# Out-projection of a hybrid attention layer by seven block products instead of eight

## The chip, the cores and the metric

The kernel runs on one core of a Trainium2 chip. The metric is the time of one execution on the device in microseconds (us); lower is better. The core has five engines that work side by side, each through its own instructions in order: PE (TensorE, matmuls), DVE (VectorE), ACT (ScalarE), POOL (GpSimd) and SP (SyncE), which here issues every DMA. An instruction waits on semaphores of other engines, and what stands behind it on its engine waits with it.

## The reference, cut to what matters

One layer: a normalised input of 2048 tokens x 1024 goes through one projection, whose columns feed an attention with 8 heads and a gated recurrence with 4 heads. Their gated outputs, 512 columns each, are joined to `y` (2048 x 1024). Then:

```
y = jnp.concatenate([y_mla, y_hg], axis=-1) @ w_out[l]
x = x + y.astype(x.dtype)
...
return rms_norm(x, final_norm_g)
```

All data are float32. Of the layer only this last product, 2048 x 1024 by 1024 x 1024, is computed in another way by the change.

## The kernel before

A matmul here takes operands of 32 bits at reduced precision (`fp32r`). To keep float32 accuracy every operand is cut in a high part (a cast, on ACT) and a low part (value minus high part, on DVE or POOL), and a product is three matmuls, high x high, high x low, low x high: the helper `mm3`, lines L68 to L70. A matmul has 128 x 128 stationary weights and up to 512 columns, so "128x512" is the largest.

The work stands in three phases. Up to some 705 us come the in-projections (weights `wr` loaded in 256 KB pieces, L196, cast and cut at L202 and L203 into `w`) with the recurrence between them. Up to 1268 us comes the attention: for each head and each 256 queries, scores (L854 to L856), softmax (L859 to L870), transposes of the probabilities (L902), their cast and cut (L905, L906), applies to the values (L920, L921), then the head's output `oa` (copied L931, L932, gated L933) stored to DRAM (`y_d`, L935). The recurrence's half of `y` had been stored to the same `y_d` earlier. Last comes the out-projection (L1010 to L1055): 16 blocks of 128 tokens, and for each a load of `yl` from `y_d` (L1020, 512 KB), cast and cut (L1021, L1022), a load of the residual `x` (L1024), two halves of 512 output columns with 8 x 3 matmuls each, an add of the residual from PSUM (L1035), the sum of squares (L1036), the product with the norm's weight (L1040) or a scaling with it (L1047), a scaling (L1046) and a store (L1052). `w_out` is loaded and cut in the last head (`load_wout`, L947 to L960, at step WOUT of that head).

The program's order on each engine is not that of the code: a scheduler simulates the program and writes instructions of every engine in the order in which they could start there. So the first blocks of the out-projection are mixed into the last steps of the attention. DMAs carry one of eight rotating semaphores (`DMAHW0` to `DMAHW7` in rows of the order); each waits for the one eight places before it.

## Time and profile before

| | |
|---|---|
| time, median of 3 runs | 1424.99 us (1424.39 to 1425.21) |
| span of the profiled execution | 1424.0 us |
| PE busy | 1395.9 us, 98% |
| DVE, ACT, POOL busy | 67%, 62%, 33% |
| first out-projection matmul, last apply of the attention, last matmul (start) | 1231.1, 1267.14, 1417.58 us |

The profiled execution is one of its own; its own time is its span, from the first to the last instruction. A share of busy time is an average over all phases. PE's listed durations overlap, since matmuls are pipelined: the time that one counts is read from the distance of starts.

### The profile page before, as it was taken

The numbers are of one execution on the slowest core, as the hardware profiler recorded it, in microseconds if no ns is written. First come the engines' busy times: TensorE is split into PE (matmuls) and PEld (weight loads), VectorE is DVE, ScalarE is ACT, GpSimd is POOL, SyncE is SP. The second block draws the span as 40 slices with busy tenths as digits, with TensorE's granted clock in tenths as the row PEclk, the third lists the DMA queues.
The fourth block names the chain that finished last, engine by engine and source line by source line (L and its number), as shares of the span: only waits on it lengthen the run. The fifth ranks groups of instructions, "written<-read, shape, count | busy, mean of one in ns | idle before, by whom it ended". The sixth has DMA issues, their size and how long they took to land.

```text
span 1424.0 us, 25891 instructions
## 1 busy us (share of the span) xinstructions
PE 1395.9 (98%) x9314; PEld 1271.8 (89%) x9314; DVE 954.6 (67%) x2433; ACT 878.6 (62%) x1796; POOL 464.3 (33%) x635
## 2 busy tenths in 40 slices
PE   8999999999999999999989999999999999999998
PEld 7899879989889988999879999999999998888887
DVE  6547855595645746658389889897889888744333
ACT  6565575456672647345387788778877888732232
POOL 3123613083121522227262425233433425411010
PEclk9999999999999999999989999999999999999999
DMA  6211211214221112111640110000010103244342
GB/s 185 75 48 46 75 52 31 70 38 157 64 60 35 45 60 74 45 42 36 165 106 9 28 23 13 22 15 20 15 27 9 25 24 100 79 137 148 133 148 104
DMA packets 96351, 92.10 MB, mean 65 GB/s; under 512 B 31072, under 2 KB 84576, under 8 KB 96096
## 3 DMA queue, kind: packets, MB, share of 16 engines
q1 hardware_dynamic: 96224, 90.46, 21.7%
q8 instruction: 73, 1.20, 0.4%
q14 instruction: 54, 0.44, 0.1%
HBM read 64.22 MB, written 25.17 MB: 63 GB/s over the span
## 4 chain that ended last, share of the span: by engine, by line
PE 86%; DVE 5%; ACT 3%; POOL 2%; DMA 2%; issue 2%; SPq 0%; POOLq 0%; DVEq 0%; ACTq 0%
PE ps_mm L68 14%; PE ps_mm L69 14%; PE ps_mm L70 14%; PE ps_tp L902 8%; PE ps_a L921 5%; PE ps_a L920 4%; PE ps_mm L854 4%; PE ps_mm L855 4%; PE ps_mm L856 4%; PE ps_b L68 2%; PE ps_b L70 2%; PE ps_b L69 2%; PE ps_b L459 1%; PE ps_a L459 1%; POOL dd L441 1%
## 5 line engine op out<-in xcount | busy, mean ns | idle before, releaser
L68 PE MATMUL ps_mm<-w,hh 128*128 128x256 f32 (+3 forms) x896 | 270.2, 302 | 0.0
L69 PE MATMUL ps_mm<-w,hh 128*128 128x256 f32 (+3 forms) x896 | 265.3, 296 | 0.0
L70 PE MATMUL ps_mm<-w,hl 128*128 128x256 f32 (+3 forms) x896 | 264.2, 295 | 0.0
L906 DVE TENSOR_TENSOR pl<-ps_tp,ph 128x512 fp32r<-128x512 f32 (+1 forms) x288 | 184.4, 655 | 32.9 <-ACT ph L905 32.3
L905 ACT CAST ph<-ps_tp 128x512 fp32r<-128x512 f32 (+1 forms) x288 | 154.1, 565 | 61.5 <-PE ps_tp L902 47.3
L68 PEld LDWEIGHTS ps_mm<-w,hh 128*128 128x128 f32 x896 | 171.4, 191 | 1.0 <-ACT kr L234 0.3
L69 PEld LDWEIGHTS ps_mm<-w,hh 128*128 128x128 f32 x896 | 171.2, 191 | 0.4
L70 PEld LDWEIGHTS ps_mm<-w,hl 128*128 128x128 f32 x896 | 170.6, 190 | 0.1
L902 PE MATMUL ps_tp<-ident,sn 128*128 128x128 f32 x1088 | 168.1, 274 | 0.6 <-ACT sn L868 0.5
L868 ACT ACTIVATE sn<-sn,mx 128x128 f32<-128x128 f32 (+15 forms) x128 | 154.6, 1208 | 21.5 <-DVE mx L863 21.0
L920 PE MATMUL ps_a<-ph,vp 128*128 128x256 f32 x576 | 155.5, 290 | 0.0
L921 PE MATMUL ps_a<-pl,vp 128*128 128x256 f32 x576 | 147.3, 289 | 0.3 <-DVE pl L906 0.2
L441 POOL TENSOR_TENSOR dd<-G 128x512 f32<-128x512 f32 x80 | 92.9, 1166 | 144.0 <-DVE qd L454 109.3
L902 PEld LDWEIGHTS ps_tp<-ident,sn 128*128 128x128 f32 x1088 | 126.9, 140 | 8.5 <-ACT sn L868 1.1
L854 PE MATMUL ps_mm<-k_hi,qh 128*128 128x512 f32 (+3 forms) x320 | 131.1, 410 | 0.3 <-DVE sn L859 0.2
L859 DVE TENSOR_SCALAR_CACHE_REDUCE sn<-ps_mm,mx 128x512 f32<-128x512 f32 (+3 forms) x192 | 111.5, 581 | 10.0 <-PE ps_mm L856 8.3
L856 PE MATMUL ps_mm<-k_hi,ql 128*128 128x512 f32 (+3 forms) x320 | 116.7, 365 | 1.2 <-DVE ql L815 1.2
L855 PE MATMUL ps_mm<-k_lo,qh 128*128 128x512 f32 (+3 forms) x320 | 116.4, 364 | 0.0
L203 DVE SCALAR_TENSOR_TENSOR w<-wr,lng,w 128x256 fp32r<-128x256 f32 (+3 forms) x168 | 88.4, 568 | 39.3 <-ACT w L202 39.3
L921 PEld LDWEIGHTS ps_a<-pl,vp 128*128 128x128 f32 x576 | 109.1, 189 | 6.1 <-DVE pl L906 1.4
L920 PEld LDWEIGHTS ps_a<-ph,vp 128*128 128x128 f32 x576 | 109.0, 189 | 5.8 <-ACT ph L905 0.4
L887 POOL TENSOR_SCALAR gp<-gate,ri 128x64 f32<-128x64 f32 x128 | 56.3, 443 | 174.1 <-DVE ri L870 158.4
(275 smaller groups left out, 3355.3 us busy)
## 6 DMA issues: line engine op xcount, KB each, us to landing
wr<-in_w_in SPq DMA_DIRECT2D x68, 256.0 KB
yl<-y_d SPq DMA_DIRECT2D x16, 512.0 KB
vp<-in_x SPq DMA_DIRECT2D x16, 512.0 KB
out<-sn SPq DMA_DIRECT2D x15, 512.0 KB
xt<-in_x SPq DMA_DIRECT2D x8, 512.0 KB
y_d<-yt SPq DMA_DIRECT2D x16, 256.0 KB
gate<-gate_d SPq DMA_DIRECT2D x8, 512.0 KB
y_d<-oa SPq DMA_DIRECT2D x64, 64.0 KB
```

The costliest lines, as they stand in the source:

```text
L68: PE.matmul(ps, l_hi, r_hi, start=start, stop=False)
L69: PE.matmul(ps, l_hi, r_lo, start=False, stop=False)
L70: PE.matmul(ps, l_lo, r_hi, start=False, stop=stop)
L854: PE.matmul(p[:, :w], qh[:, qs], kh[:, ks], start=True, stop=False)
L855: PE.matmul(p[:, :w], qh[:, qs], kl[:, ks], start=False, stop=False)
L856: PE.matmul(p[:, :w], ql[:, qs], kh[:, ks], start=False, stop=True)
L868: A.activation(sn[:, :nk], sn[:, :nk], AF.Exp, bias=mx[:, kc:kc + 1], scale=-1.0, accum_out=rs)
L902: PE.transpose(tp[:, o:o + 128], prow[i][:, (kb + u) * 128:(kb + u + 1) * 128], ident)
L905: A.copy(ph[:, :w], tp[:, :w])
L906: V.tensor_tensor(pl[:, :w], tp[:, :w], f32(ph[:, :w]), ALU.subtract)
L920: PE.matmul(dst, vv, ph[:, rng], start=st_, stop=False)
L921: PE.matmul(dst, vv, pl[:, rng], start=False, stop=en)
```

## The change

Strassen's scheme in Winograd's form: two blocks of 128 tokens are a pair (8 pairs), `y` of a pair is cut in four quadrants a11, a12, a21, a22 (128 tokens x 512), `w_out` in b11 to b22 (512 x 512). Seven products of sums of quadrants replace eight. The sums of weights are t1 to t4, those of `y` are s1 to s4. Sums of products are not added up by an engine: products accumulate on in PSUM. A first product in bank a is copied by ACT to bank b, the third product is added there, and that is copied on to bank c; a, b, c and e then take further products and DVE adds the banks to the residual. Two matmuls at the start only initialise banks b and c.

`wout_sums` makes the weight sums, in 8 calls for 128 rows x 256 columns of each quadrant: 2 loads of `w_out`, 4 subtracts on POOL, 3 casts on ACT, 3 subtracts on DVE, 7 stores to `w_d` in DRAM. The code hangs the calls on the in-projections. In the last head `load_wout` loads b11, t1, t2, b21, t3, already cut (10 loads of 1 MB); `load_late` loads pair 0's `y` (as `vp`) and b22 and t4 uncut. After the attention pair 0's `y` is loaded a second time (`yr`) into a new pool `op`, for the operands a12, s3, s4 and a22. Tiles of the attention (`ks`, `vs`, `qf`, `qh`, `ql`) move to the pool `big`, which closes at `load_late`. The core of the diff:

```
-WOUT = 4
+WOUT = 3
...
+    def wout_sums(kk, ch):
...
+        ns = slice(ch * 256, ch * 256 + 256)
+        wr = st.tile([128, 2, 2, 256], F32, tag="ws", bufs=1, name="ws")
+        for g in range(2):
+            r0 = g * 512 + kk * 128
+            DMA.dma_start(wr[:, g], w_out[r0:r0 + 128, :].rearrange("p (c n) -> p c n", c=2)[:, :, ns])
+        t = st.tile([128, 2, 256], F32, tag="wt", bufs=1, name="wt")
+        G.tensor_tensor(t[:, 0], wr[:, 0, 1], wr[:, 0, 0], ALU.subtract)
+        G.tensor_tensor(wr[:, 0, 1], wr[:, 1, 1], wr[:, 0, 1], ALU.subtract)
+        DMA.dma_start(w_d["b22"][:, kk, ns], wr[:, 1, 1])
+        G.tensor_tensor(wr[:, 1, 1], wr[:, 1, 1], t[:, 0], ALU.subtract)
+        G.tensor_tensor(t[:, 1], wr[:, 1, 0], wr[:, 1, 1], ALU.subtract)
+        DMA.dma_start(w_d["t4"][:, kk, ns], t[:, 1])
+        for src, names in ((wr[:, :, 0], ("b11", "b21")), (wr[:, :, 1], ("t3", "t2")), (t[:, 0:1], ("t1",))):
+            hl = st.tile([128, 2, 2, 256], F32R, tag="whl", bufs=2, name="whl")
+            n = len(names)
+            A.copy(hl[:, 0, :n], src)
+            V.tensor_tensor(hl[:, 1, :n], src, f32(hl[:, 0, :n]), ALU.subtract)
+            for i, name in enumerate(names):
+                DMA.dma_start(f32(w_d[name][:, :, kk, ns]), f32(hl[:, :, i]))
...
-    merge(U[7:], lat_q(0, hA))
+    merge(U[7:], lat_q(0, hA), sums[0:2])
...
+        return [ops[0], lambda: late("b22", w_d["b22"]),
+                lambda: late("t4", w_d["t4"])] + ops[1:4]
...
+    def late_split(name, kk):
+        hi, lo = wset[name]
+        A.copy(hi[:, kk], f32(lo[:, kk]))
+        G.tensor_tensor(lo[:, kk], f32(lo[:, kk]), f32(hi[:, kk]), ALU.subtract)
...
+    order = (("a11", "b11", "a"), ("s1", "t1", "e"), ("s2", "t2", "b"), ("a12", "b21", "a"),
+             ("s3", "t3", "b"), ("s4", "b22", "c"), ("a22", "t4", "b"))
...
+        def product(i, ns=slice(0, 512)):
+            a, w, bk = order[i]
+            (ah, al), (wh, wl), p = o[a], wset[w], acc[bk][:, ns]
+            for k in range(4):
+                first = i < 2 and k == 0
+                PE.matmul(p, ah[:, k], wh[:, k, ns], start=first, stop=False, skip_group_check=True)
+                PE.matmul(p, ah[:, k], wl[:, k, ns], start=False, stop=False, skip_group_check=True)
+                PE.matmul(p, al[:, k], wh[:, k, ns], start=False, stop=k == 3, skip_group_check=True)
...
+            if i == 0:
+                A.copy(acc["b"], acc["a"])
+            elif i == 1:
+                add(0, H1, acc["e"])
+                add(1, H1, acc["e"])
+            elif i == 2:
+                A.copy(acc["c"], acc["b"])
+            elif i == 3:
+                add(0, H0, acc["a"])
+                done(0, H0, True)
...
+    ys = [{} for _ in range(NBLK // 2)]
+    ys[0] = outs["y0"]
+    rest = operands(0, ys[0])
+    run(rest[:2])
+    rest = rest[5:]
+    run(rest[:1])
+    for name in ("b22", "t4"):
+        for kk in range(4):
+            late_split(name, kk)
+    run(rest[1:])
+    for b in range(NBLK // 2):
+        more = operands(b + 1, ys[b + 1]) if b + 1 < NBLK // 2 else []
+        merge(pair_products(b, ys[b]), more)
```

How the order on the engines moves, first SP early, right after the loads of the rotary tables' inputs (`pi`, `iv`). Names as above; in brackets the semaphores waited for. Before:

```order
L544 DMA pi<-in_positions 128x16x1 [waits DMAHW6_49]
L548 DMA iv<-in_c_inv 128x16 [waits DMAHW7_49]
L196 DMA wr<-in_w_in 128x2x256 [waits DMAHW2_49,DMAHW0_49,DVE_49]
L159 DMA xt<-in_x 128x1024 [waits DMAHW1_49,PE_49]
L159 DMA xt<-in_x 128x1024 [waits DVE_49,PE_49]
```

After (`ws`, `wt`, `whl` are the tiles of `wout_sums`, `wd_...` their places in DRAM):

```order
L551 DMA iv<-in_c_inv 128x16 [waits DMAHW7_49]
L596 DMA ws<-in_w_out 128x2x256 [waits DMAHW0_49]
L596 DMA ws<-in_w_out 128x2x256 [waits DMAHW1_49]
L199 DMA wr<-in_w_in 128x2x256 [waits DMAHW2_49,DVE_49]
L600 DMA wd_b_102<-ws 128x256 [waits DMAHW3_49,DMAHW1_49]
L610 DMA wd_b_96<-whl 256x1x256 [waits DMAHW4_49,DVE_49]
L610 DMA wd_b_99<-whl 256x1x256 [waits DMAHW5_49]
L603 DMA wd_t_101<-wt 128x256 [waits DMAHW6_49,Pool_49]
L610 DMA wd_t_100<-whl 256x1x256 [waits DMAHW7_49,DVE_49]
```

The 72 DMAs of the eight calls fill SP from here up to the stores of the rotary tables (`cs_d`), with the loads `wr` and `xt` between them.

Second, PE at the last applies of the attention. Before:

```order
L68 MATMUL ps_mm<-wo_hi_15277,yh 128x512
L921 MATMUL ps_a<-pl,vp 128x256 [waits DVE_49]
L920 MATMUL ps_a<-ph,vp 128x256
L921 MATMUL ps_a<-pl,vp 128x256
L920 MATMUL ps_a<-ph,vp 128x256 [waits Activation_49]
L921 MATMUL ps_a<-pl,vp 128x256 [waits DVE_49]
L920 MATMUL ps_a<-ph,vp 128x128
L921 MATMUL ps_a<-pl,vp 128x128
L69 MATMUL ps_mm<-wo_lo_15278,yh 128x512
```

After (L949 and L950 are the applies, L1153 to L1155 the three matmuls of a product):

```order
L949 MATMUL ps_a<-ph,vp 128x256 [waits Activation_49]
L950 MATMUL ps_a<-pl,vp 128x256 [waits DVE_49]
L949 MATMUL ps_a<-ph,vp 128x128
L950 MATMUL ps_a<-pl,vp 128x128
L1153 MATMUL ps_mm<-b21s,ah 128x512 [waits DMAHW2_49,Activation_49]
L1154 MATMUL ps_mm<-b21s,ah 128x512
L1153 MATMUL ps_mm<-t3s,ah 128x512 [waits DMAHW4_49,Activation_49]
L1154 MATMUL ps_mm<-t3s,ah 128x512
L1155 MATMUL ps_mm<-b21s,al 128x512 [waits DVE_49]
```

Before, matmuls of the out-projection stand among the applies and right behind them. After, the last eight groups of transposes and applies have none between them, and the next is the fourth product, whose `ah` comes from `yr`.

Third, SP at the same place. Before:

```order
L1024 DMA vp<-in_x 128x1024 [waits DMAHW6_49]
L935 DMA y_d_72<-oa 64x256 [waits DMAHW3_49,Pool_49]
L1020 DMA yl<-y_d_69 128x8x128 [waits PE_49]
L1024 DMA vp<-in_x 128x1024 [waits DMAHW5_49,PE_49]
L1052 DMA out<-sn 128x1024 [waits DVE_49,Activation_49]
L935 DMA y_d_72<-oa 64x256 [waits DMAHW7_49,Pool_49]
```

After:

```order
L1013 DMA b22l<-wd_b_102 128x2048 [waits DMAHW3_49]
L1013 DMA t4l<-wd_t_101 128x2048 [waits DMAHW4_49,PE_49]
L964 DMA y_d_72<-oa 64x256 [waits DMAHW5_49,Pool_49]
L964 DMA y_d_72<-oa 64x256 [waits DMAHW6_49,Pool_49]
L1121 DMA fng<-in_final_norm_g 128x1024 [waits DMAHW7_49,DVE_49]
L1029 DMA yr<-y_d_69 128x8x256 [waits DMAHW0_49,PE_49]
L1141 DMA xt<-in_x 128x1024 [waits DMAHW1_49]
```

The load of the next `y` stood before the attention's last store; now it stands behind it and behind the load of the norm's weight.

## Rows read from the trace of the kernel before

**Rows 1.** The page, part 1: busy us (share of the span) xinstructions of each engine

```profile
PE 1395.9 (98%) x9314; PEld 1271.8 (89%) x9314; DVE 954.6 (67%) x2433; ACT 878.6 (62%) x1796; POOL 464.3 (33%) x635
```

**Rows 2.** Windows, 1231 to 1400: us, busy by engine, granted clock, DMA share, GB/s

```profile
1231.00:1400.00 169.00, 169.00 (x798) 141.69 (x797) 67.27 (x107) 55.49 (x108) 20.29 (x34) 1.00 0.40 133
```

**Rows 3.** Timeline of PE: start us, us, engine, line, operation, out<-in; eight in a row

```profile
1289.77 0.39 PE L69 MATMUL ps_b<-wo_lo,yh 128*128 128x512 f32 x1
...
1291.36 0.39 PE L70 MATMUL ps_b<-wo_hi,yl 128*128 128x512 f32 x1
```

**Rows 4.** Timeline of PE, the last two matmuls

```profile
1417.45 0.28 PE L69 MATMUL ps_b<-wo_lo,yh 128*128 128x256 f32 x1
...
1417.58 0.28 PE L70 MATMUL ps_b<-wo_hi,yl 128*128 128x256 f32 x1
```

**Rows 5.** Groups by line, 1190 to 1425: xcount | busy us, mean ns | idle before

```profile
L1022 DVE TENSOR_TENSOR yl<-yl,yh 128x1024 fp32r<-128x1024 f32 x16 | 20.0, 1248 | 26.3 <-ACT yh L1021 26.3
L1036 ACT ACTIVATE sn<-vp 128x512 f32<-128x512 f32 x31 | 19.6, 632 | 88.0 <-DVE vp L1035 84.0 <-PE ps_tp L902 4.0
...
L1021 ACT CAST yh<-yl 128x1024 fp32r<-128x1024 f32 x16 | 16.7, 1050 | 13.0 <-DMA yl<-y_d 13.0
...
L1035 DVE TENSOR_TENSOR vp<-ps_mm,vp 128x512 f32<-128x512 f32 x21 | 14.5, 688 | 24.8 <-PE ps_mm L70 22.5 <-DMA vp<-in_x 2.1
...
L1047 DVE SCALAR_TENSOR_TENSOR sn<-vp,rxp,ks 128x512 f32<-128x512 f32 x16 | 12.0, 751 | 10.7 <-POOL rxp L1045 10.7
```

**Rows 6.** Timeline at the attention's end; in brackets idle time before, and its releaser

```profile
1267.14 0.27 PE L921 MATMUL ps_a<-pl,vp 128*128 128x128 f32 x1
...
1267.45 0.37 ACT L931 COPY oa<-ps_a 64x256 f32<-64x256 f32 x1 [1.27 <-PE ps_a L921]
...
1267.83 0.75 DVE L1047 SCALAR_TENSOR_TENSOR sn<-vp,rxp,ks 128x512 f32<-128x512 f32 x1 [0.68 <-POOL rxp L1045]
...
1268.49 0.41 DVE L932 TENSOR_TENSOR oa<-ps_a,oa 64x256 f32<-64x256 f32 x1
...
1269.04 0.74 POOL L933 TENSOR_TENSOR oa<-oa,og 64x256 f32<-64x256 f32 x1 [1.25 <-issue]
...
1270.11 0.34 SPq L1052 DMA_DIRECT2D out<-sn  x1
...
1270.54 0.45 SPq L935 DMA_DIRECT2D y_d<-oa  x1
```

**Rows 7.** Timeline: issue of a load of y, and the cast that it releases

```profile
1247.44 0.37 SPq L1020 DMA_DIRECT2D yl<-y_d  x1
...
1251.35 1.05 ACT L1021 CAST yh<-yl 128x1024 fp32r<-128x1024 f32 x1 [0.37 <-DMA yl<-y_d]
```

**Rows 8.** Windows, 0 to 20 and 20 to 118

```profile
0.00:20.00 20.00, 15.22 (x78) 11.59 (x79) 9.98 (x26) 13.38 (x26) 9.35 (x30) 0.83 0.92 298
20.00:118.00 98.00, 97.50 (x645) 88.69 (x644) 54.56 (x115) 59.30 (x101) 15.71 (x16) 1.00 0.23 59
```

**Rows 9.** Windows with a granted clock under 1

```profile
152.40:155.80 3.40, 3.40 (x15) 3.11 (x14) 3.40 (x10) 3.00 (x12) 2.13 (x4) 0.50 0.00 0
710.00:715.00 5.00, 1.56 (x7) 1.28 (x8) 3.33 (x5) 2.90 (x7) 4.52 (x5) 0.72 1.04 302
715.00:720.00 5.00, 3.77 (x12) 2.51 (x10) 5.00 (x8) 4.72 (x10) 4.45 (x4) 0.50 0.78 201
720.00:725.00 5.00, 4.46 (x12) 3.49 (x13) 3.71 (x16) 4.34 (x10) 3.42 (x6) 0.50 1.30 244
```

**Rows 10.** Groups of POOL by line, 20 to 118

```profile
L441 POOL TENSOR_TENSOR dd<-G 128x512 f32<-128x512 f32 x10 | 11.6, 1158 | 40.7 <-DVE qd L454 32.1 <-DVE kd L453 4.6 <-PE ps_a L430 2.3
```

**Rows 11.** Timelines of ACT's casts of w_in and of SP's loads of it

```profile
42.72 2.52 ACT L202 ACTIVATE w<-wr,lng 128x256 fp32r<-128x256 f32 x6 [3.69 <-PE ps_mm L70]
...
63.26 0.51 ACT L202 ACTIVATE w<-wr,lng 128x256 fp32r<-128x256 f32 x1
...
44.18 1.18 SPq L196 DMA_DIRECT2D wr<-in_w_in  x2
```

More of the change, by code (lines that the diff above doesn't have):

```diff
@@ L584, in run @@
             f()
+    def wout_sums(kk, ch):
[18 more added lines that the diff above has]
+                DMA.dma_start(f32(w_d[name][:, :, kk, ns]), f32(hl[:, :, i]))
+    sums = [lambda kk=kk, ch=ch: wout_sums(kk, ch) for kk in range(4) for ch in range(2)]
     hA, itA = zip(*[load_h(c) for c in range(2)])
@@ L645, in hybrid_kernel @@
     merge(U[:16], vv + gg)
[L646 removed]
+    merge(U[16:], lat_q(1, hB), sums[4:6])
     raws, fq, vv, gg = hg_proj(1, hB)
@@ L650, in hybrid_kernel @@
     merge(U[:16], vv + gg)
-    merge(U[16:], lat_kv(1, hB))
+    merge(U[16:], lat_kv(1, hB), sums[6:8])
     run(gates(1, hB))
@@ L943, in stage_b, with wtile @@
         return items
-    w_hi, w_lo = [], []
+    wset = {}
+    def wtile(pool, name):
+        t = pool.tile([128, 2, 4, 512], F32R, name=name + "s")
+        wset[name] = (t[:, 0], t[:, 1])
+        return t
     def load_wout():
@@ L949, in load_wout @@
         wo = p2r.enter_context(tc.tile_pool(name="wo", bufs=1, side="right"))
-        for k2 in range(KT // 2):
-            wr = wk.tile([128, 2, D], F32, tag="vp", name="vp")
-            DMA.dma_start(wr, w_out[k2 * 256:(k2 + 1) * 256, :].rearrange("(k p) n -> p k n", p=128))
-            for j in range(2):
-                k = 2 * k2 + j
-                a = wo.tile([128, D], F32R, name=f"wo_hi{k}")
-                b = wo.tile([128, D], F32R, name=f"wo_lo{k}")
-                A.copy(a, wr[:, j])
-                (V if k == 0 else G).tensor_tensor(b, wr[:, j], f32(a), ALU.subtract)
-                w_hi.append(a)
-                w_lo.append(b)
+        tiles = {}
@@ new lines, in part, with load_late, late @@
+        def part(name, kk):
+            if kk == 0:
+                tiles[name] = wtile(wo, name)
+            DMA.dma_start(f32(tiles[name][:, :, kk:kk + 2]), f32(w_d[name][:, :, kk:kk + 2]))
+        return [lambda name=name, kk=kk: part(name, kk) for name in EARLY for kk in (0, 2)]
+    ln = ExitStack()
+    outs = {}
+    def load_late():
+        p2k.close()
+        pool = ln.enter_context(tc.tile_pool(name="ln", bufs=1, side="right", reuse_waits="tile"))
+        outs["y0"] = y0 = {}
+        ops = pair_operands(0, y0, lambda: wk.tile([128, KT, 256], F32, tag="vp", name="vp"),
+                            lambda: pool.tile([128, 4, 128], F32, tag="ss0", bufs=2, name="ss0"),
+                            lambda: (pool.tile([128, 4, 128], F32R, tag="ah0", bufs=3, name="ah0"),
+                                     pool.tile([128, 4, 128], F32R, tag="al0", bufs=3, name="al0")))
+        def late(name, src):
+            hi = pool.tile([128, 4, 512], F32R, name=name + "h")
+            lo = pool.tile([128, 4, 512], F32R, name=name + "l")
+            wset[name] = (hi, lo)
+            DMA.dma_start(f32(lo), src)
+        return [ops[0], lambda: late("b22", w_d["b22"]),
+                lambda: late("t4", w_d["t4"])] + ops[1:4]
@@ new lines, in late_split, with pair_operands, load, split @@
+    def late_split(name, kk):
+        hi, lo = wset[name]
+        A.copy(hi[:, kk], f32(lo[:, kk]))
+        G.tensor_tensor(lo[:, kk], f32(lo[:, kk]), f32(hi[:, kk]), ALU.subtract)
+    def pair_operands(b, o, ytile, stile, otile):
+        def load():
+            o["raw"] = ytile()
+            c, t0 = b // 2, (b % 2) * 256
+            DMA.dma_start(o["raw"], y_d[c][:, t0:t0 + 256].rearrange("(k p) t -> p k t", p=128))
+        def split(name, src):
+            hi, lo = o[name] = otile()
+            A.copy(hi, src)
+            V.tensor_tensor(lo, src, f32(hi), ALU.subtract)
+        def quad(g, i):
+            return o["raw"][:, 4 * g:4 * g + 4, i * 128:(i + 1) * 128]
+        def total(name, x0, x1, op):
+            t = o["f" + name] = stile()
+            V.tensor_tensor(t, x0, x1, op)
+        def first():
+            split("a11", quad(0, 0))
+        def second():
+            total("s1", quad(0, 1), quad(1, 1), ALU.add)
+            split("s1", o["fs1"])
+        def third():
+            total("s2", o["fs1"], quad(0, 0), ALU.subtract)
+            split("s2", o["fs2"])
+        def fourth():
+            split("a12", quad(1, 0))
+        def fifth():
+            total("s3", quad(0, 0), quad(0, 1), ALU.subtract)
+            split("s3", o["fs3"])
+        def sixth():
+            total("s4", quad(1, 0), o["fs2"], ALU.subtract)
+            split("s4", o["fs4"])
+        return [load, first, second, third, fourth, fifth, sixth, lambda: split("a22", quad(1, 1))]
```

134 lines of the change are left out of this document (86 added, 48 removed).

## The prediction

> **What bounds the kernel now.** I read the page's busy times first [rows 1]: TensorE (PE) works 1395.9 of the 1424.0 us, 98%; VectorE has 67%, ScalarE 62%, GpSimd 33%. An average can hide a stage with another limit, so next I read the stretch that the change rewrites, from 1231 us, where the out-projection begins, to 1400 [rows 2]: PE 169.00 of 169.00 us, VectorE 67.27, ScalarE 55.49, DMA share 0.40. There only PE's work counts. How much one matmul counts is read from starts, since the listed durations overlap [rows 3]: from 1289.77 to 1291.36 lie seven steps, 0.227 us for each 128x512 matmul. The 256-wide ones at the very end follow each other at 0.13, 0.12 over the whole last cut [rows 4]. From the last one's start at 1417.58 to the end at 1424.0 runs a tail of 6.4 us (add, square, power, scale, store), which both kernels have in the same form; I cost it at nothing.
>
> **The matmuls removed.** Before: 16 blocks x 2 halves x 24 = 768 matmuls, 48 of them 256 wide: 744 x 0.227 + 48 x 0.12 = 174.6 us. After: 8 pairs x 7 products x 12 = 672, the last product's 12 cut into 24 of 256, and two that only initialise banks: 662 x 0.227 + 24 x 0.12 = 153.2. That is **-21.5 us**, if PE stays as full as now. The Trainium skill (TensorE: Matmul & The Clock Gate, "Back-to-back issue gap") gives 512 / 2.4 + 2.5 = 216 ns for such a step; the rows show 227, so the skill's figure would make the term an estimated -20.5, and I go by the rows.
>
> **Whether the other engines keep up.** A pair of blocks has 84 x 0.227 = 19.1 us of PE. VectorE gets per pair 7 subtracts of 128x512 (half of a 1024-wide one's 1.248: 0.62), 4 totals of the same kind, 6 adds from PSUM (0.69), 2 products with the norm's weight (taken like an add) and 2 scalings (0.75) [rows 5]: 6.9 + 4.1 + 2.9, with small ones 14.5 us. ScalarE: 7 casts (half of 1.050: 0.53), and 4 squares, 2 scalings and 2 PSUM copies, all at the square's 0.63 [rows 5]: 8.8 us. Both are under 19.1, so I cost steady state at nothing. A copy from bank a to b has product 1's 2.7 us to hide in; if that cover were gone it would cost 0.6 us per pair.
>
> **The end of the attention.** This is where the order turns against the change. Before, out-projection matmuls of several blocks fill PE between the last softmax groups, and SP has later loads ready. After, only pair 0's first three products (36 matmuls, 8.2 us) and the initialisers can run there. The fourth needs a12, which is cut out of a second load of pair 0's y into another pool, and this load stands on SP's queue behind the last store of the attention's output and the load of the final norm's weight. The store waits for a chain that I follow in the rows of before [rows 6]: last apply on PE at 1267.14, ScalarE's copy 1267.45 (0.37), VectorE 0.41, GpSimd 0.74, then SP's issue 0.45. Left undisturbed (in before a scaling of 0.75 on VectorE and an output store stood between) that is 2.0 us to the store's issue and 2.5 us to the next one. Then 0.5 MB of norm weight and 1 MB of y must land. A 0.5 MB load of y took from 1247.44 until ScalarE could start at 1251.35, 3.9 us [rows 7]; at the 298 GB/s of the busiest early stretch [rows 8] its bytes are 1.75 us, so some 2.2 us are fixed; 1.5 MB make 5.0 + 2.2 = 7.2. Then a cast (0.53) before the first matmul, and two totals and a subtract (1.9) before the first low half; four matmuls fill a part of that. Sum: 2.5 + 7.2 + 0.5 + 0.5 = **+10.5 us** in which PE has nothing. Bounds: 7, if the norm weight lands meanwhile (1.7 less) and no fixed part is paid twice; 13, if the transfer runs at the 201 GB/s of another crowded stretch [rows 9]. The 36 matmuls ahead of it were counted already; the gap is idle time on top of them. Queued behind the same load on SP are four loads of x (2 MB, 7 us); pair 1's y comes after them and lands some 10 us behind the first, while pair 0's last four products take 10.9, so nothing more is late.
>
> The eight last softmax groups now run without filler. A group has four 256-wide applies and four transposes half as wide; at the 0.12 of a 256-wide step [rows 4], which bounds the narrower one too, that is at most 1.0 us of PE, and I take 0.9; a cast and a subtract of a group end to end are 1.2 [rows 5]. If each group waits for its own, 8 x 0.3 = 2.4; if the three PSUM banks overlap them, nothing. I take **+1**.
>
> **The clock.** PE's granted clock fell at the one long idle time that before shows, the start of the attention: it is 0.72 in 710 to 715, 0.50 in 715 to 720 and 720 to 725 (1.2 instead of 2.4 GHz) [rows 9]. A dense stretch also ran at 0.50 from 152.40 to 155.80, with PE busy throughout [rows 9]. At half clock PE does half: the short dip costs 1.7 us, two and a half such 5 us slices would cost 6. The restart after the gap is dense (matmuls are queued with weights in place), so it is nearer to the short dip: **+2.5**, bounds 1.7 and 6. The Trainium skill warns of just this edit's pattern (TensorE: Matmul & The Clock Gate, "HAM oscillation — how this bites in real kernels"): matmul bursts separated by DMA waits are each restarted cold. The rows agree that an idle PE restarts at half clock; by the Trainium skill's rule the cost would come at each such wait, here at one.
>
> **The sums, early.** The eight weight-sum calls depend on nothing, and the order puts all of them between the first load for the rotary tables and the stores of the tables, about 20 to 118 us of before, though the code hangs them later. There PE is busy 97.50 of 98.00 us, ScalarE 59.30, VectorE 54.56, GpSimd 15.71, at 59 GB/s [rows 8]. Added: 32 GpSimd operations of 128x256 (half of 1.158 us each [rows 10]) 18.5 us; 16 casts of 512 and 8 of 256 on ScalarE 10.6; their subtracts on VectorE 12.4; 72 DMAs, at 0.4 to 0.6 us of SP each some 35 us; 16.8 MB. The stretch then moves 22.6 MB in 98 us, 230 GB/s, under the 298 that rows show; no engine gets full. w_in's loads share that queue, but they run far ahead: one issued at 44.18 lies until the casts from 63.26 on [rows 11], 19 us, against some 10 us for a dozen sum DMAs. So their cover is that lead. Bounds: 0, and 14, if the DMAs run at 201 GB/s (112 us for 98). I take **+2**, near the lower end, since room and lead are both there. The loads in the last head (10 loads of 1 MB of split weights; each waits for the one eight before it) have from 1190 to the first product at 1231, 41 us, and need 34 to 37; hidden. b22's and t4's splits are done before pair 0 needs them.
>
> **Sum:** -21.5 + 10.5 + 1 + 2.5 + 2 = -5.5. The profiled run's span is 1424.0, 1.0 under the median of the runs shown (1424.99); against the median: **1419.5 us**.
>
> **Rivals.**
> (a) *The gap is mostly covered*: y lands sooner, or the attention's tail stretches under the fillers so that the load is issued before PE runs out. For it: the load itself needs only data written long ago; against it: its place behind the store. With a gap of 3 and a clock that holds: -21.5 + 3 + 1 + 2 = -15.5, about 1409.
> (b) *The early loads come late* (the one that ends slower): ScalarE waits in order for a weight-sum's load, evictions and w_in's casts stand behind it, PE stops and loses clock each time. Place: 20 to 118 us. Price: the bound of 14 and two dips of 1.7 in place of 2: -21.5 + 14 + 14 + 3.4 = +9.9, about 1435. It decides from 7.5 us of early stall on. Against it: ScalarE at 70 of 98 us and 19 us of lead.
> (c) *VectorE bounds the out-projection*: needs 14.5 to exceed 19.1, operations a third dearer than their rows; at 40% dearer 1.2 x 8 = +10, about 1429.
> (d) *The clock stays down after the gap* as long as at the attention's start: 6 in place of 2.5, or, with a second stop behind it, more: 1423 to 1425. By the Trainium skill's rule named above a second stop would again restart cold.
>
> **How the numbers follow.** Chances: the forecast (1415 to 1422) 0.45, (a) 0.17, (b) 0.17, (c) 0.07, (d) 0.09, and 0.05 for a shift of a few us either way at the attention's start, whose tiles now lie in another pool. A measurement of this kernel tells 0.2% (2.85 us) from no change. Faster takes the forecast, (a) and some of the last: 0.65. Same: half of (d), of (c) and of the last, and (b)'s milder part: 0.17. Slower: the rest of (b), (c), (d): 0.18. The range goes from (a), 1407, to the milder half of (b) and (c), 1429; the forecast's own is 1415 to 1422.
>
> **What would show it.** Right: 84 matmuls a pair at 0.227 us, an idle PE of 7 to 13 us after the last apply ended by the DMA of yr, a granted clock of 0.5 behind it, PE over 97% busy from 20 to 118 us. Wrong: PE waits for ScalarE there with a loading w or ws behind it (b); pairs longer than 19.1 us with VectorE full (c); no gap (a).

## The result and the profile after

The changed kernel takes 1474.92 us (median, 1471.62 to 1476.39), the kernel before 1424.76 on the same chip: a ratio of 1.0344 [1.0331, 1.0357]. I had forecast 1419.5. Its profiled run has a span of 1473.7 us, 49.7 more than before.

The page of the changed kernel, busy times, answers to [rows 1]:

```profile
PE 1395.6 (95%) x9208; PEld 1261.7 (86%) x9208; DVE 1017.2 (69%) x2544; ACT 911.5 (62%) x1876; POOL 483.8 (33%) x668
```

PE has about a hundred matmuls fewer and is as long busy as before, though now for 95% of a longer span. So the work that went was made up by slower or half-clocked work, and the 49.7 us are time in which PE stood (50 us more of idle time than before). Where, the starts tell: I set the start of each PE instruction beside that of the same instruction in before.

| place (us of before) | delay of the changed kernel |
|---|---|
| to 45 | 0 |
| 87, 100, 124 | +8.5, +13.9, +18.7 |
| 157 to 690 | +20.6 |
| 726 to 1194 (the attention) | +29.0 |
| end | +49.7 |

Three places, then: the early sums, the attention's start, the out-projection. The windows of the changed kernel over them (columns as in [rows 2]; [rows 8] has the first of them in before, 97.50 of 98.00 us):

```profile
20.00:118.00 98.00, 88.56 (x517) 76.75 (x517) 59.35 (x113) 60.17 (x107) 34.98 (x41) 0.95 0.65 201
735.00:740.00 5.00, 0.00 (x0) 0.00 (x0) 2.70 (x6) 0.73 (x1) 3.02 (x2) 0.50 0.69 168
745.00:750.00 5.00, 4.53 (x13) 3.05 (x13) 3.10 (x5) 3.09 (x7) 1.96 (x2) 0.50 0.95 184
1246.00:1254.00 8.00, 0.39 (x2) 0.00 (x0) 0.29 (x2) 1.66 (x3) 0.45 (x1) 0.69 0.76 299
1254.00:1262.00 8.00, 7.44 (x44) 7.21 (x45) 3.83 (x7) 3.89 (x9) 1.45 (x2) 0.68 0.03 8
1298.00:1306.00 8.00, 4.26 (x10) 3.33 (x11) 4.87 (x8) 2.37 (x4) 0.00 (x0) 0.50 0.90 346
1320.00:1400.00 80.00, 74.52 (x313) 59.19 (x312) 53.58 (x90) 35.53 (x71) 8.56 (x13) 0.98 0.46 158
```

**The early sums.** PE's waits from 20 to 130 us (line waited for: us in total, times, longest):

```profile
PE ps_mm L68 <- ACT w L205: 5.4, 3, 3.1
PE ps_mm L70 <- DVE w L206: 2.1, 2, 1.5
```

PE waits for the casts of w_in (L205, L202 of before). ScalarE's own waits from 40 to 160 us say why those are late:

```profile
ACT whl L607 <- DMA ws<-in_w_out: 17.1, 5, 4.4
...
ACT whl L607 <- POOL ws L601: 6.0, 3, 2.9
...
ACT whl L607 <- DMA wd_b<-whl: 2.8, 3, 1.6
```

L607 is the cast of a weight sum. It stands in ScalarE's order ahead of casts of w_in and evictions of PSUM, and waits 17.1 us for its load, 6.0 for GpSimd, 2.8 for a buffer that is still being stored. VectorE in turn waits for it (L608, the subtract behind the cast: 30.5 us), with subtracts of w_in behind. The casts of w_in themselves wait only 2.2 us for their own loads here, 4.3 in before: these loads are not late. PE's listed waits from 20 to 160 us add up to 12.6 us (2.3 in before). The granted clock was 0.50 in 71.5 to 78.1 and 102.2 to 105.4, with 8.3 us of PE busy in it: an estimated 4.1 us more. That is some 14 of the 20.6; the rest no view here accounts for.

**The attention's start.** In before PE waited here for 3.3 us (timeline of PE of before, in the low clock of [rows 9]):

```profile
714.41 0.80 PE L68 MATMUL ps_b<-c_hi,wk_hi 128*128 128x512 f32 x1 [3.29 <-ACT ks L799]
```

Now it is 13.0. The timelines of ACT, PE and SP of the changed kernel:

```profile
744.35 0.58 ACT L828 COPY ks<-ps_b 64x512 f32<-64x512 f32 x1 [3.09 <-DMA gate_d<-gt]
```

```profile
744.99 0.79 PE L68 MATMUL ps_b<-c_hi,wk_hi 128*128 128x512 f32 x1 [13.02 <-ACT ks L828]
```

```profile
729.92 9.82 SPq L791 DMA_DIRECT2D gate<-gate_d  x2
739.85 1.62 SPq L342 DMA_DIRECT2D gate_d<-gt  x1
```

The copy into `ks` waits for a store of `gate_d`: the tile now lies over the buffer that this store reads, and the store stands on SP behind two loads that took 9.8 us to issue.

**The out-projection.** PE's waits from 1225 to 1470:

```profile
PE ps_mm L1153 <- ACT ah L1033: 10.8, 1, 10.8
PE ps_a L949 <- DVE oa L961: 8.0, 1, 8.0
PE ps_mm L1153 <- ACT ps_mm L1192: 5.7, 2, 3.9
PE ps_mm L1155 <- DVE al L1034: 5.0, 4, 1.6
```

The first is the forecast gap, from the last apply's end at 1290.97 on. Its place in the timelines of SP, ACT and PE:

```profile
1293.25 0.54 SPq L1121 DMA_DIRECT2D fng<-in_final_norm_g  x1
1293.88 0.41 SPq L1029 DMA_DIRECT2D yr<-y_d  x1
```

```profile
1301.06 0.62 ACT L1033 CAST ah<-yr 128x512 fp32r<-128x512 f32 x1 [9.68 <-DMA yr<-y_d]
1301.73 0.80 PE L1153 MATMUL ps_mm<-b21s,ah 128*128 128x512 f32 x1 [10.76 <-ACT ah L1033]
```

The second is not in the prediction. SP, ACT and PE at the first output of the last head behind the weights' loads:

```profile
1232.86 4.79 SPq L992 DMA_DIRECT2D t3s<-wd_t  x1
1237.74 2.29 SPq L964 DMA_DIRECT2D y_d<-oa  x1
```

```profile
1253.47 0.37 ACT L960 COPY oa<-ps_a 64x256 f32<-64x256 f32 x1 [6.18 <-DMA y_d<-oa]
1254.35 0.58 PE L949 MATMUL ps_a<-ph,vp 128*128 128x256 f32 x1 [7.95 <-DVE oa L961]
```

There are two `oa` tiles. Their stores stand on SP behind 10 MB of split weights, so the third output finds no free tile, and the next applies no free bank. Waits three and four are in the pairs: a bank copy and a low half that come late, 10.7 us together. Below, a stop that is not read from such waits is given as the distance of two starts, which is some 0.3 to 0.4 us more than the idle time.

The step from one 512-wide matmul to the next, which [rows 3] has at 0.227 us, is here 1.64 / 7 = 0.234 (timeline of PE, seven steps):

```profile
1370.14 0.40 PE L1153 MATMUL ps_mm<-b21s,ah 128*128 128x512 f32 x1
...
1371.78 0.39 PE L1154 MATMUL ps_mm<-t1s,ah 128*128 128x512 f32 x1
```

VectorE's dearest groups of the pairs, 1310 to 1470, are close to what was costed from [rows 5] (0.69 for an add, 0.62 for a subtract):

```profile
L1159 DVE TENSOR_TENSOR xt<-ps_mm,xt 128x512 f32<-128x512 f32 (+1 forms) x38 | 25.3, 674 | 22.4 <-PE ps_mm L1155 21.6 <-DMA xt<-in_x 0.8
...
L1034 DVE TENSOR_TENSOR al<-ss,ah 128x512 fp32r<-128x512 f32 x28 | 18.7, 683 | 5.8 <-ACT ah L1033 5.8
```

### The profile page after: what moved, and what is told of

Same layout as the page of the kernel before. It is cut to its first block, busy times and chain, and to the rows that moved or that the text cites. A ratio compares the mean times of both kernels' runs of the same rounds, so it can differ in the third digit from the quotient of the medians.

```text
span 1473.7 us, 26068 instructions
## 1 busy us (share of the span) xinstructions
PE 1395.6 (95%) x9208; PEld 1261.7 (86%) x9208; DVE 1017.2 (69%) x2544; ACT 911.5 (62%) x1876; POOL 483.8 (33%) x668
## 4 chain that ended last, share of the span: by engine, by line
PE 69%; DVE 9%; DMA 9%; ACT 5%; issue 3%; POOL 3%; SPq 1%; POOLq 0%; ACTq 0%; DVEq 0%
PE ps_mm L68 9%; PE ps_mm L69 9%; PE ps_mm L70 9%; PE ps_tp L931 8%; PE ps_a L950 5%; PE ps_a L949 4%; PE ps_mm L883 4%; PE ps_mm L885 4%; PE ps_mm L884 4%; DMA yr<-y_d 2%; DMA ws<-in_w_out 2%; PE ps_mm L1155 2%; PE ps_mm L1153 2%; PE ps_mm L1154 2%; PE ps_b L462 1%
## 5 line engine op out<-in xcount | busy, mean ns | idle before, releaser
L949 PE MATMUL ps_a<-ph,vp 128*128 128x256 f32 x576 | 157.5, 293 | 8.0 <-DVE oa L961 8.0
L950 PE MATMUL ps_a<-pl,vp 128*128 128x256 f32 x576 | 149.0, 291 | 0.0
L949 PEld LDWEIGHTS ps_a<-ph,vp 128*128 128x128 f32 x576 | 110.1, 191 | 13.2 <-DVE oa L961 8.6
L950 PEld LDWEIGHTS ps_a<-pl,vp 128*128 128x128 f32 x576 | 110.2, 191 | 5.5 <-DVE pl L935 1.0
L206 DVE SCALAR_TENSOR_TENSOR w<-wr,lng,w 128x256 fp32r<-128x256 f32 (+3 forms) x168 | 88.7, 571 | 33.7 <-ACT w L205 33.5
```

What stands on the lines that cost most here:

```text
L949: PE.matmul(dst, vv, ph[:, rng], start=st_, stop=False)
L950: PE.matmul(dst, vv, pl[:, rng], start=False, stop=en)
```

## Experiments

Theory: three separate queues in order (ScalarE behind a sum's load, `ks` behind a store, outputs behind weights) and the pairs' own waits make up the loss. Rivals: traffic, engine time, or one delay that the others follow from. Each ratio is to runs of before on the same chip, with a 95% interval; the changed kernel's own is 1.0344 [1.0331, 1.0357].

**e1_before_sums**: before, with the eight sum calls and nothing else of the change.

```diff
-    merge(U[7:], lat_q(0, hA))
+    merge(U[7:], lat_q(0, hA), sums[0:2])
```


> The kernel before with the eight weight-sum calls added in the changed kernel's places (same loads, subtracts, casts and stores; the sums are stored and never read), out-projection as before. Theory (the early sums alone cost the early shift of 20.6 us that the matched matmuls of the two traces show between 45 and 157 us): 1445, give or take 2, with the shift at the same places. Rival (the early shift comes from other parts of the change, the sums are hidden in the engines' free time): 1425 to 1428.

1442.9 us, 1.0133 [1.0118, 1.0149]; delay +17.5 at 122 us and +19.3 from 152 on. ScalarE's waits there, as in the changed kernel:

```profile
ACT whl L607 <- DMA ws<-in_w_out: 16.7, 6, 4.4
```
The sums alone cost 18.4 us: the theory held.

**e11_stores**: the change with all of the sums' stores, and loads, casts and subtracts of one call alone.

```diff
+        if not same:
...
+            same["hl"], same["wr"] = hl, wr
+        hl, wr = same["hl"], same["wr"]
```


> The changed kernel with the stores of the eight calls alone: one pair of tiles is loaded, cast and cut, and stored to all 56 places (the weight sums are left out, so the weights are wrong). Theory (the early cost is ScalarE standing in order in front of loads and subtracts, not the traffic): most of the 18 to 20 us is gone, 1475 - 16 = 1459. Rival (the traffic on SP and on the DMA engines makes the loads of w_in late): 1470 to 1475.

1454.94 us, 1.0202 [1.0178, 1.0227], 20 us under the change; the delay is 4.0 at most (140 us) and +1.4 from 250 on. The window 20 to 118:

```profile
20.00:118.00 98.00, 95.77 (x624) 85.59 (x622) 53.08 (x110) 57.36 (x99) 14.88 (x15) 1.00 0.62 193
```
The same traffic (193 GB/s beside 201) costs next to nothing. It is the sums' work and waiting in the engines' order, not the bytes.

**e5_pin**: the change, with each call's loads held back behind the recurrence's state at its place in the code.

```diff
+        G.tensor_copy(wr[:, :, 0, 0:1], state[0][:, 0:2].unsqueeze(2))
```


> The changed kernel with each weight-sum call tied to the recurrence's state at its place in the code (a copy of two columns of the state into the tile before its loads), so that the eight calls lie in two groups of four, some 120 to 200 and 450 to 550 us, in place of one run of eight from 20 on. Theory (the 18 to 20 us come from ScalarE standing in order in front of loads of a crowded run, with the casts of w_in behind it): spread out the calls cost 5 or less, 1475 - 15 = 1460. Rival (each call costs its 2.3 to 2.6 us wherever it lies, since its own load and subtracts are always waited for): 1472 to 1475.

1465.7 us, 1.0286 [1.0268, 1.0304]: 9 us under the change, between the two. The delay is +8.7 at 181 us, +7.5 at 400, +14.2 at 566 (+20.5 in the change): moved into a later stretch, four calls cost 7 us all the same.

**e2_before_big**: before, with `ks`, `vs`, `qf`, `qh`, `ql` in the pool that the change gives them.

```diff
-                stash["k"] = wk.tile([64, S], F32, tag="ks", bufs=1, name="ks")
+                stash["k"] = big.tile([64, S], F32, tag="ks", bufs=1, name="ks")
```


> The kernel before with only the move of ks, vs, qf, qh, ql and the pool big as in the changed kernel. Theory (the 8.5 us at the attention's start come from ks lying over the buffer whose store to gate_d has not been made yet, since that store stands behind the gate loads on SP): 1433, with the wait on ScalarE's copy of ks of some 13 us in place of 3. Rival (the wait at the attention's start comes from the sums' delay of other loads, the pool does nothing): 1425.

1432.52 us, 1.0061 [1.0044, 1.0078], and PE's wait for `ks` (timeline):

```profile
721.40 0.80 PE L68 MATMUL ps_b<-c_hi,wk_hi 128*128 128x512 f32 x1 [11.32 <-ACT ks L799]
```
The pools alone cost 8 us by the medians (5.8 by the two profiles).

**e8_pools**: the change, with the left pools of the first phase opened in another order, so that another buffer lies under `ks`.

```diff
+    st = p1.enter_context(tc.tile_pool(name="st", bufs=2, side="left"))
     hp_ = p1.enter_context(tc.tile_pool(name="hp", bufs=2, side="left"))
     wp = p1.enter_context(tc.tile_pool(name="wp", bufs=10, side="left"))
-    st = p1.enter_context(tc.tile_pool(name="st", bufs=2, side="left"))
```


> The changed kernel with the three left pools of the projections opened in another order (st, hp, wp), by which the pool big no longer lies over the tile gt. Theory (from the kernel before with the moved tiles: 8 us at the attention's start are the wait of ks for the stores of gt): 1475 - 8 = 1467. Rival (another tile waits for the same stores): 1473 to 1475.

1471.2 us, 1.0325 [1.0305, 1.0345]. In its profile the wait for `ks` is back at 2.8 us and the delay grows there from 20.5 to 22.7 (the change: 29.0), so the cause is met. But the stop for `oa` grew from 8.0 to 9.6, the out-projection's part of the delay from 20.7 to 23.2, and of the 8 us the medians show 3.7, not clear of the change's interval.

**e7_oa6**: the change with six `oa` tiles instead of two.

```diff
-            tmp = wk.tile([64, 256], F32, tag="oa", name="oa")
+            tmp = wk.tile([64, 256], F32, tag="oa", bufs=6, name="oa")
```


> The changed kernel with six buffers for the attention's output oa in place of two. Theory (the 8 us stop at 1246 us, with half clock behind it, is the output's buffer, whose store to y_d stands behind 10 MB of weights): the stop goes, 8 + some 5 of clock, 1475 - 13 = 1462. Rival (PE then reaches the first product before its weights and y have landed, and waits there instead): 1470 to 1475.

1462.35 us, 1.0258 [1.0239, 1.0278], 12.6 under the change. PE's waits have no L949 any more. Not all of the 12.6 is the stop's: by the profiles 4.2 of it lie ahead of the last head (+24.8 at 1194 instead of +29.0), where the `oa` tiles play no part. From there to the last apply 11.7 are gained, the stop of 8.0 and the clock behind it; 3.6 of these are lost again in the pairs, where the clock was granted at 0.50 in three stretches (1349.8 to 1353.0, 1394.1 to 1397.3, 1438.5 to 1441.7) and in the change in one (1365.1 to 1368.4). So the stop with its clock is worth 8 to 12 us.

**e3_one_load**: pair 0's y loaded once, ahead of the attention's last stores.

```diff
-        ops = pair_operands(0, y0, lambda: wk.tile([128, KT, 256], F32, tag="vp", name="vp"),
+        ops = pair_operands(0, y0, lambda: pool.tile([128, KT, 256], F32, name="raw0"),
...
-    run(rest[:2])
+    run(rest[1:2])
```


> The changed kernel with pair 0's y loaded once, into the pool that stays open, and all seven operands cut from it. Theory (the idle 10.8 us after the last apply is the second load of y behind the attention's last store): that idle time goes, and with it the half-clock restart, 1475 - 10.8 - 2.7 = 1461. Rival (the single load, which now waits for the end of the scores, only moves the wait to the first product): 1470 to 1475.

1471.75 us, 1.0333 [1.0317, 1.0348]: 3 us by the medians, not clear of the change's interval. The stop of 11.0 shrinks to 1.3 and 0.9, and pair 1's first product stops for 6.6 us instead, for a y that is still issued behind the last store. The wait was handed on.

**e4_yr2**: the change with two buffers for y.

```diff
-        items = pair_operands(b, o, lambda: op.tile([128, KT, 256], F32, tag="yr", name="yr"),
+        items = pair_operands(b, o, lambda: op.tile([128, KT, 256], F32, tag="yr", bufs=2, name="yr"),
```


> The changed kernel with two buffers for y of a pair in place of one. Theory (the stalls inside the pairs, 4.3 + 2.2 + three times 1.75 us and half clock behind the first, come from the load of the next pair's y, which waits until all operands of the last are cut): 1475 - 13 = 1462. Rival (the operands' ring of eight buffers holds the cuts back, so the load comes no sooner in effect): 1472 to 1475.

1470.72 us, 1.032 [1.0294, 1.0345]: 4 us by the medians, the intervals overlapping. The stops in the pairs go from 4.30, three of 1.98 and 2.24 to 2.37, 1.07 and 2.24: the second buffer met its cause, and the time gained less than the stops did.

**e9_all**: these repairs together, with the norm's weight in the late weights' pool and the next pair's y issued ahead of the residuals.

```diff
+        outs["fng"] = pool.tile([128, D], F32, name="fng")
...
+    nxt = [operands(b, ys[b]) for b in range(1, NBLK // 2)]
+    run(nxt[0][:1])
+    run(rest[1:2])
```


> The changed kernel with the three edits of this call and the two of the call before together (pinned sums, six buffers for oa, pools in the other order, pair 0's y loaded once, two buffers for the pairs' y), and the norm's weight loaded with b22 and the next pair's y issued ahead of the residuals. Theory (five separate causes, each gone): 1475 - 15 - 13 - 8 - 11 - 8 = 1420, under the kernel before by a little. Rival (the waits hand on what is saved, as one load of y alone did): 1435 or more.

1442.13 us, 1.0116 [1.0098, 1.0133], with a new stop: PE's waits from 1225 on begin with

```profile
PE ps_mm L1155 <- DVE xt L1161: 8.1, 3, 5.9
```
Now the adds wait for pair 0's residual. The out-projection is level with before's (+19.3 at the end, +19.4 at 1194); what is left stands ahead of it, +14.6 from the sums and some 5 at the attention's start.

**e10_pool** and **e10_spread**: e9_all with the sum calls at eight places instead of four and pair 0's residual issued ahead of pair 1's y; in e10_pool the sums' casts and subtracts also on GpSimd.

```diff
-            A.copy(hl[:, 0, :n], src)
-            V.tensor_tensor(hl[:, 1, :n], src, f32(hl[:, 0, :n]), ALU.subtract)
+            G.tensor_copy(hl[:, 0, :n], src)
+            G.tensor_tensor(hl[:, 1, :n], src, f32(hl[:, 0, :n]), ALU.subtract)
```


> The kernel with all edits together, the eight sums now one by one at eight places of the projections and with their casts and subtracts on GpSimd in place of ScalarE and VectorE, and pair 0's residuals loaded ahead of pair 1's y. Theory (what is left of the sums' cost is ScalarE's and VectorE's time and waits in order, and the 6.3 us stop at pair 1 is the add that waits for the residual): 1442 - 8 - 4 = 1430. Rival (GpSimd, which makes the recurrence's differences, becomes the one that is waited for): 1440 to 1450.

> As the run on GpSimd, but with casts and subtracts on ScalarE and VectorE as in the changed kernel. Theory (one call at a place costs some 1 us, four in a row cost 7): 1442 - 5 - 4 = 1433. Rival (each call costs the same 1.8 us wherever it stands): 1438.

e10_pool 1438.33 us, 1.009 [1.0075, 1.0106]; e10_spread 1448.95, 1.0164 [1.0147, 1.0181]. Spread on ScalarE the calls cost what they cost in e9_all (delay +14.6 at 566 us); on GpSimd the delay is -0.5 there and +3.5 at 690. So spreading does nothing, and taking the calls out of ScalarE's and VectorE's order gives back most of it. The other edit of both, the residual ahead of pair 1's y, had been put at -4 and cost 4: the out-projection's part of the delay goes from 0 in e9_all to +4.2 and +3.9, with stops of 4.7 and 4.3 for pair 1's y and of 4.2 at a bank copy.

**e12_layout**: before, with w_out and y cut in tiles as in the change.

```diff
+            yh = op.tile([128, 4, 128], F32R, tag=f"yh{g}", name="yh")
```


> The kernel before with w_out and y in tiles cut as in the changed kernel (512-wide blocks of w_out, y in two halves of 4 x 128), the product the same as before. One theory (the steps of 0.233 us in place of 0.227 come from how the operands lie in the tiles): the out-projection's steps become 0.233 and the time 1430. Rival (they come from the products' order and from accumulating on in four banks, or from the other engines' load): steps of 0.227, 1425.

1426.61 us, 1.0007 [0.9994, 1.0021]; the step stays at 226.7 ns. Not the tiles' shape.

**e13_shift** and **e16_shift64**: before, with 96 or 64 unused bytes behind yh and yl, which moves their place.

```diff
         yl = op.tile([128, KT, 128], F32R, tag="yl", name="yl")
+        if b == 0:
+            op.tile([128, 24], F32, name="pad", bufs=1)
```
(16 in place of 24 in e16_shift64)

> Kernel before, with 96 unused bytes per partition in the pool of yh and yl, so that the stationary operand of the out-projection's matmuls lies 96 bytes off the moving one's position modulo 512, as it does in the change (in before the two lie at the same position). Theory (the pace hangs on where the two operands lie to each other): the 512-wide step of the out-projection goes from 226.7 ns to the change's 233.3, and 744 of them make it about +5 us, 1431. Rival (the slower pace of the change comes from the traffic on PSUM and the other engines around it, not from the addresses): the step stays at 226.7 and the time at 1426.

> Kernel before with 64 unused bytes instead of 96. In both traces the 512-wide steps whose operands lie 64 bytes apart modulo 256 take 228.6 ns on average, those 96 apart 234 and those 192 apart 233.6. Theory (classes of positions, 64 among the good ones): the step stays within 2 ns of 226.7 and the time at 1426 to 1427. Rival (any offset costs): 233 and 1431.

e13: 1430.57 us, 1.0032 [1.0019, 1.0044], mean step 233.3 ns, the changed kernel's. In the timeline seven steps now take 1.63 us:

```profile
1370.06 0.39 PE L69 MATMUL ps_mm<-wo_lo,yh 128*128 128x512 f32 x1
...
1371.69 0.40 PE L70 MATMUL ps_mm<-wo_hi,yl 128*128 128x512 f32 x1
```
e16: 1427.35, 1.0014 [1.0006, 1.0023], mean step 228.9. So the place of the stationary operand sets the pace: 64 bytes cost a third of what 96 do. Neither expectation for 64 holds as put: 228.9 is 2.2 over before's step, and it is what that expectation has for steps of this offset in the two traces (228.6).

**e14_align**: the change, with 96 bytes that bring its operands to the same place.

```diff
+    op.tile([128, 24], F32, name="pad")
```


> The change, with the same 96 unused bytes ahead of the tiles of the out-projection's pool, so that the high and low parts of y lie at the weights' position modulo 512. Theory (addresses): the step goes from 233.3 to 226.7 ns, 672 of them give -4.5 us, about 1470; the stops stay. Rival (traffic): the step stays at 233.3 and the time at 1475.

The step is 226.8 ns, as the theory has it; the time is 1475.7, 1.035 [1.0334, 1.0366], as the rival has it. From the end of the gap on its profile gains nothing on the change's (+1.0 us). The pairs' stops grew (a new one of 1.75, three of 2.07 where 1.98 stood, 4.43 for 4.30): quicker matmuls wait longer for the same casts. That is some 2 of the 4.4 us. Clock took about as much again: it was granted at 0.89 in 1356 to 1386, behind the bank copy's stop, and at 0.96 in 1386 to 1470, where the change has 0.94 and 0.98 in the stretches 5 us later.

**e15_best**: e10_pool with the 96 bytes, pair 1's y loaded into the late weights' pool ahead of the last stores (for room one buffer fewer for pair 0's low halves there), and the norm's weight behind pair 0's residual.

```diff
+            outs["raw1"] = pool.tile([128, KT, 256], F32, name="raw1")
+            DMA.dma_start(outs["raw1"], y_d[0][:, 256:512].rearrange("(k p) t -> p k t", p=128))
```


> The change with all its repairs so far (the first pin, the sums on GpSimd and spread, six output tiles, the pools' order, one load of pair 0's y, two buffers for y), and new: the 96 bytes that align the operands, and pair 1's y loaded into the late weights' pool ahead of the attention's last stores, with the norm's weight loaded behind pair 0's residual instead. From 1438.3: theory (the rest of the loss is the stop of 4.7 us for pair 1's y with the 4.3 us for the bank copy behind it, some 3 us of clock, and 4.5 us of pace): about 1423, level with before or just under it. Rival (the waits are handed on once more, to the residual or the norm's weight): only the pace comes back, about 1434.

1428.06 us, 1.0019 [1.001, 1.0027]: between the two. One large stop is left, 6.2 us at 1261.36, behind this cast (timeline of ACT):

```profile
1266.91 0.62 ACT L1041 CAST ah<-raw 128x512 fp32r<-128x512 f32 x1 [4.88 <-DMA y_d<-oa]
```

**e17_order**: e15_best with another tile over the attention's last outputs.

```diff
     run(nxt[0][:1])
+    run(nxt[1][:1])
```


> The kernel of e15_best with one thing changed: pair 2's y is taken first from the out-projection's pool, so that this tile, and not pair 0's high part of a12, lies where the attention's last output tiles were. In e15_best ScalarE waited 4.9 us there for the last store of y_d to finish, and PE stood 6.2 us. Theory: that stop shrinks to 1 to 2 us and some 2 us of clock come back: 1428.1 - 4.5 - 2, about 1421.5, under before (1425.7). Rival (the wait is handed on to the adds, which need pair 0's residual, issued behind the same store): the stop reappears a product or two later, 1427.

1431.43 us, 1.0036 [1.0022, 1.0049]: the rival was right. That stop is 1.25 now, and one of 5.1 stands at 1272.77, where PE's next product waits for an add, and that for pair 0's residual. The timeline of GpSimd shows what delayed the last store, and so the residual behind it:

```profile
1263.68 4.73 POOL L963 TENSOR_TENSOR oa<-oa,og 64x256 f32<-64x256 f32 x1 [2.69 <-DVE oa L962]
```

**e18_gate**: e17_order with this one operation on VectorE.

```diff
-            G.tensor_tensor(tmp, tmp, gs, ALU.mult)
+            (V if (h, j) == seq[-1] else G).tensor_tensor(tmp, tmp, gs, ALU.mult)
```


> The kernel of e17_order with the gate of the attention's very last output on VectorE instead of GpSimd. In e17_order that one GpSimd operation of 64x256 took 4.73 us, where the same operation takes 0.76 on average in the attention of before, while VectorE ran seven operations back to back beside it; the last store and pair 0's residual stood behind it and PE stood 4.7 us for the first add. Theory: the store and the residual come some 4 us earlier, that stop goes, the clock stays up behind it (0.79 in 1276 to 1300 of e17_order): 1431.4 - 4.5 - 2.5, about 1424.5, level with before (1425.5). Rival (the residual is late by its place behind the attention's buffers, not by GpSimd's operation): the stop stays at 4 to 5 us and the time at 1431.

**1423.51 us**, 0.9982 [0.9968, 0.9996]: the theory held, and this is the one version with seven products that comes out under before, by less than the 0.2% that a measurement can tell. The operation takes 0.42 us (timeline of DVE), the stop at the adds went from 5.1 to 2.7, and the pairs run as forecast (window):

```profile
1263.92 0.42 DVE L963 TENSOR_TENSOR oa<-oa,og 64x256 f32<-64x256 f32 x1
```

```profile
1320.00:1400.00 80.00, 79.95 (x350) 65.12 (x350) 54.68 (x92) 38.34 (x78) 8.18 (x17) 1.00 0.41 144
```
By its profile (a run of 1427.79 us) the delay is +4.0 at 690, +11.0 at 1194 and +2.0 at the end. So the out-projection is 9 us shorter than before's, and the sums and the attention's start still cost 11.

## Why the prediction was wrong

**The step that failed first, and the largest one, is "The sums, early".** I took +2 with a bound of 14; it is 18.4 alone and 20.6 in the change. That is the mechanism of rival (b), which I had given 0.17, and its price there, 14 and 3.4 of clock, was close. What misled me is how I bounded it: I compared bytes, GpSimd's and ScalarE's busy time and SP's issue time with the stretch, found room in each, and took the 14 from the transfer rate. e11_stores shows that the transfers cost next to nothing. The cost is who stands behind the waiting cast on ScalarE, and behind its subtract on VectorE: casts of w_in, their subtracts and PSUM evictions, for which PE waits. The 19 us of lead that I named as cover is in the loads of w_in, and these were not late (2.2 us of waits); it is the casts and subtracts behind them that were held up, and PE's waits for L205 and L206 show that these have no such lead.

**Three things had no term, or zero.** The pools at the attention's start: +8 (8.4 in the starts; e2_before_big 8), in the prediction a case of 0.05 "of a few us either way". The attention's stores behind the weights: I costed the 10 MB against the weights' own deadline, "hidden", and did not ask what SP would issue after them; 8.0 us of stop, 8 to 12 with its clock (e7_oa6). "So nothing more is late" in the pairs: 10.7 us of stops, some 6 of them from one buffer for y (e4_yr2); that the rest are bank copies in ScalarE's order is read from PE's waits, no run takes them out.

**Pace.** 0.227 us per step was read from before and carried over. It is 0.2333 in the change: 662 steps of 6.6 ns, +4.4 us of PE's work. The cause is shown (the operands' place, e13_shift, e14_align), though e14_align also shows that the change as it is would not have gained by it.

**What was right.** The matmuls: with stops and pace repaired, 80 us of the out-projection are full at 0.227 (e18_gate), so the -21.5 was real work removed (the prediction's words say 768 matmuls with 48 of 256; its sum rightly has 744 + 48 = 792), though e18_gate with its last stops keeps 9 of it. The gap: 10.5 forecast, 10.8 measured, at the place and with the releaser named, and its parts fit too: 2.5 from the last apply to the issue of the norm's weight (2.3 measured), 7.2 from there until ScalarE can start (7.8), 0.5 for the cast (0.7) and 0.5 for the low half, for which PE did not wait. VectorE and ScalarE keep up, so rival (c) is out; (a) too, since the gap is there.

**The clock.** Behind the gap it was granted at 0.50 from 1298 to 1306. Twelve matmuls took 5.28 us there (1301.73 to 1307.01), against their usual 0.233 us an estimated 2.5 more, as forecast. But the stop for `oa` cost clock as well (0.69 and 0.68 in 1246 to 1262), and so did the pairs' longest, 3.9 us, which 0.50 follows at 1365. The others of the pairs, 1.6 to 1.8 us, were followed by a clock of 1.00 in the change (1400 to 1466) and twice by one of 0.50 in e7_oa6. The Trainium skill (TensorE: Matmul & The Clock Gate, "HAM oscillation — how this bites in real kernels") has bursts between waits for DMAs restart cold each time. This trace agrees at its three longest stops of the out-projection (8.0, 10.8 and 3.9 us), and not at the short ones. What rival (d) had put as "a second stop behind it" came ahead of the gap and behind it. Windows of the changed kernel, the three places at 0.50 and the stretch with the short stops:

```profile
1254.30:1259.20 4.90, 4.86 (x23) 4.86 (x23) 1.85 (x3) 2.18 (x5) 0.72 (x1) 0.50 0.06 13
1301.75:1306.95 5.20, 5.20 (x12) 4.05 (x13) 4.29 (x8) 1.75 (x3) 0.00 (x0) 0.50 0.67 255
1365.10:1368.40 3.30, 3.30 (x9) 2.58 (x8) 2.86 (x7) 0.00 (x0) 1.53 (x1) 0.50 0.14 56
1400.00:1466.00 66.00, 60.46 (x264) 48.00 (x263) 35.76 (x62) 26.01 (x56) 7.43 (x14) 1.00 0.31 112
```

In the out-projection the forecast was -21.5 + 10.5 + 1 + 2.5 = -7.5; measured is 49.7 - 29.0 = +20.7. Of the 28.2 between, the stop for `oa` is 8.0, the pairs 10.7, the pace 4.4, the gap 0.3. Of the 4.8 that are left the clock explains an estimated 4: PE was busy at 0.50 for 4.9 us behind the stop for `oa` and for 3.3 us at 1365, and half of that is lost.

## What to carry to other kernels

Before you put work into a gap, list for every added instruction that waits on a DMA what stands behind it on its engine, and how soon another engine needs that; bytes and busy time say nothing about it. The same goes for a queue: a long block of loads is hidden only if nothing behind it is wanted. And a repaired wait is often handed on: here most repairs, e3_one_load, e8_pools, e9_all and e17_order among them, laid bare the next late load or tile, and only the last brought the time level with before's.
